# A two-layer decoder trunk on one core: which instructions keep their written order, and where lambda and 1/rms stand

## The chip, the cores and the metric

One NeuronCore of a Trainium2 chip runs the whole kernel. The metric is device microseconds (us) of one execution; before the change it is 1796.87 us, the median of 3 runs (1796.75 to 1797.68). The engines are called as the profile calls them: PE (TensorE, matmul), DVE (VectorE), ACT (ScalarE), POOL (GpSimd), and SP, whose queue issues nearly all DMA transfers.

## The reference, cut to what matters

```python
for l in range(DEPTH):                       # 2 layers, 512 tokens, width 1024
    h = rmsnorm(x, attn_norm[l])
    proj = h @ w_in[l]
    q_a, kv_a, g_a, q_b, k_b, v_b, uv_c = jnp.split(proj, IN_OFFSETS, axis=-1)
    o_a = nsa_attention(...)                 # compressed, selected and window branches
    o_b = diff_attention(...)                # two softmax maps per head, p0 - lam * p1
    o_c = chunked_sgu(uv_c, ...)             # u * (W_s @ rmsnorm(gelu(v)) + b)
    gates = sigmoid(h @ w_merge[l] + b_merge[l])
    x = x + (sum of gates * (o @ w_branch)) @ w_out[l]
    h = rmsnorm(x, ffn_norm[l])
    x = x + (silu(h @ w_ffn1[l]) * (h @ w_ffn3[l])) @ w_ffn2[l]
return rmsnorm(x, final_norm)
```

In `diff_attention`, `lam = exp(sum(lq1*lk1)) - exp(sum(lq2*lk2)) + lambda_init`, and q and k get rotary positions (tables of cosine and sine).

## The kernel before, in words

**Tiling.** Activations lie transposed: 8 tiles of 128 channels by 512 tokens. Weights stream from HBM as chunks of 128x1024 (`wr`, 4 buffers, L146). Each chunk is split in two fp32r halves: ACT makes the high part `wh` (L163), DVE or POOL the low part `wl` (L166), 3 buffers each. Every product takes three matmuls: `wh`·x high (L184), `wl`·x high (L185), `wh`·x low (L186); the lines L224 to L226 are the same where tokens are the output rows. Without the chunk's `wl` PE gets past one matmul of it only. An output bank in PSUM (`ps_g`, 3 buffers, or `ps_s`, 2) is free again when DVE or ACT has evacuated it.

**Start.** `setup` loads x and the first chunks and makes the split inputs `xg`. ACT squares the token-major copy of x (L311); `norm_r` turns the sums into 1/rms (`v` on DVE L482, `r` by a power on POOL L483); `norm_bcast` spreads it by four transposes on PE (L489) and a copy on ACT (L492) into `R`, by which every evacuation multiplies. The matmuls themselves don't need `R`.

**First tasks of a layer**, in the written order: `kvc` (chunks 0 and 1: compression inputs k and v), `u0`, `u1`, `u2` (chunks 2 to 4), `wk0` (chunk 5: 8 matmuls of the compression, lines L563 and L564), `u3` (chunk 6), `wk1` (chunk 7), `vv0` (chunk 8), and so on. In layer 0 the evacuations of `kvc` and `u0` are put off until `R` exists. The evacuation of k makes `xr` (L531), `xp` (L543) and the two halves `xh` (ACT L547, DVE L548), which `wk0` needs; that of v does the same again. `gelu_u` multiplies by `R` on DVE (L509) and applies gelu on ACT (L510). `loads` (called in `u1`) issues the SGU and compression constants (gn, sw, sgb, w2; L1297 to L1302) and in layer 0 also `loads2` (positions, the second parameter block `par`, and `lq`, L319 to L322). `setup2` computes lambda (`ex` L355 and L358, `nl`, `bh`, `sub`) and then the cosine and sine tables; it is written after `u3`.

**What sets the order.** The Python code writes the instructions; the framework's scheduler then orders each engine's queue, and may draw an instruction ahead of ones written earlier if nothing forbids it. Each engine works its queue off in that order. `pin` forbids: on DVE, ACT and POOL it chains every instruction from `first` on to the one before it. Before the change it is called once, after `u2` of layer 0, for all instructions since the first loads.

**The value task.** `V` (three chunks, four `ps` banks of 280 columns) ends in `v_evac`: per token tile ACT writes `v` high (L692) and the gates `ga` (L693), DVE `v` low (L694). The next task, a gate of branch c, needs the first of these banks. Nothing pins this place before the change. Near it stands the softmax of the compressed branch: its Exp on ACT (L795), then DVE's L799 to L806.

Of the kernel before, what the change touches and what calls it, by code (L numbers as in the profile page):

```python
# [80 lines left out]
class Kern:  # L81
    def __init__(self, tc, ctx, A):
        self.tc, self.nc, self.A = tc, tc.nc, A
        self.sb = ctx.enter_context(tc.tile_pool(name="sb", bufs=1))
        self.ps = ctx.enter_context(tc.tile_pool(name="ps", bufs=1, space=PSUM))
        self.dr = ctx.enter_context(tc.tile_pool(name="dr", bufs=1, space=DRAM))
        self.pending, self.timed = [], []
        self.now = self.clock = 0
        self.done = set()
        self.order = []  # L90
        self.raw, self.split = {}, {}
        self.n_dma = self.n_split = 0
# [141 lines left out]
    def setup(self):  # L234
# [32 lines left out]
        self.first = len(nc.cur_bb.bb.instructions)  # L267
# [45 lines left out]
        self.mark = len(nc.cur_bb.bb.instructions)  # L313

    def loads2(self):
# [3 lines left out]
        nc.sync.dma_start(self.pos_t, A["pos"])  # L319
        nc.sync.dma_start(self.par[1], A["par"][1])  # L320
# [24 lines left out]
    def setup2(self):  # L345

        nc = self.nc
        lq = self.lq.rearrange("p (l f d) -> p l f d", l=L, f=4)
        self.nlam, self.bh, self.sub = [], [], []
        for l in range(L):  # L350
            li = 0.8 - 0.6 * math.exp(-0.3 * l)
            ex = self.const(f"ex{l}", [P, 2])
            junk = self.t2("junk", (P, HD))
            for j in range(2):
                nc.vector.tensor_tensor_reduce(out=junk, in0=lq[:, l, 2 * j], in1=lq[:, l, 2 * j + 1],  # L355
                                               scale=1.0, scalar=0.0, op0=OP.mult, op1=OP.add,
                                               accum_out=ex[:, j:j + 1])
            nc.scalar.activation(ex, ex, AF.Exp)  # L358
            nl = self.const(f"nl{l}", [P, 1])
            nc.vector.scalar_tensor_tensor(nl, ex[:, 1:2], li, ex[:, 0:1], op0=OP.subtract, op1=OP.subtract)  # L360
            self.nlam.append(nl)
            bh = self.const(f"bh{l}", [P, 24])
            nc.vector.tensor_scalar(bh, self.par[l][:, P_BM:P_BM + 24], 0.5, None, op0=OP.mult)
            self.bh.append(bh)
            sub = self.const(f"sub{l}", [P, 1])
            nc.vector.tensor_scalar(sub, self.par[l][:, P_SUB:P_SUB + 1], 1.0 - li, None, op0=OP.mult)
            self.sub.append(sub)
        yield

# [71 lines left out]
        for j, tab in enumerate((self.cosT, self.sinT)):  # L441
            for h in range(4):
                nc.sync.dma_start(tab[32 * h:32 * h + 32, :], tab_d[j].rearrange("a b c -> a (b c)"))
        yield
# [242 lines left out]
    def v_evac(self, t, ps):  # L687
        nc = self.nc
        r = self.r4[:, t:t + 1]
# [6 lines left out]
        if t == TT - 1:  # L696
            nc.vector.tensor_scalar(self.ga, self.ga, 1.0, 0.5, op0=OP.add, op1=OP.mult)
# [569 lines left out]
    def layer_tasks(self, l):  # L1267
# [21 lines left out]
        def loads():  # L1289
            if l == 0:  # L1290
                self.loads2()
# [39 lines left out]
        def g_u(m):  # L1331
            hooks, ev = {}, self.gelu_u(m)
            if l == m == 0:
                ev = lambda ps, f=self.gelu_u(0): self.later(1002, lambda: f(ps), "ev")
            elif m == 1:
                hooks = {3: loads}
                if l == 0:
                    hooks.update({1: self.norm_bcast, 2: lambda: self.ensure("ev")})
            add("u%d" % m, [("u", m)], lambda i0: self.fm(i0, [ev], self.xg, hooks=hooks,
# [94 lines left out]
    def run(self):  # L1434
# [36 lines left out]
        for n, chunks, f, need in tasks:  # L1471
# [18 lines left out]
            if n == "u20":  # L1490
                self.pin(self.first, len(self.nc.cur_bb.bb.instructions))
        self.ensure()

# [104 lines left out]
```

## Time and profile before

| | before |
|---|---|
| median of 3 runs | 1796.87 us |
| profiled execution, its own time | 1797.58 us |
| its span in the profile | 1795.8 us (1.8 us lie around it) |
| PE busy | 1766.5 us, 98% of the span |
| DVE busy | 967.8 us, 54% |
| ACT busy | 748.5 us, 42% |
| POOL busy | 385.9 us, 21% |
| mean granted clock of PE | 0.995 of full speed |

PE's busy time and the span differ by some 29 us; that is all the time in which PE stood still. Matmuls of the trace overlap (the start of the next one lies before the modelled end of the last), so rates are read from start to start.

### The profile page before, as it was taken

To read this page: it belongs to the slowest core of one execution; us is meant where nothing else is said; L and a number is where in the kernel's file an instruction comes from. 1 tells how busy PE (TensorE), PEld (TensorE's weight loads), DVE (VectorE), ACT (ScalarE), POOL (GpSimd) and SP (SyncE) were. 2 spreads that over 40 slices of the span, in tenths; PEclk is the share of its full clock that TensorE was granted. 3 is DMA by queue.
4 is the path that set the end of the run, shared out by engine and by line. 5 is a ranking of instruction groups with operands and counts; after the bars stand their busy time and mean duration, and the time that the engine had idled before them with its cause. 6 is when DMAs were issued, how large, how long until landed. Compare 5 with 4: busy or idle time off the path is not lost.

```text
span 1795.8 us, 22823 instructions
## 1 busy us (share of the span) xinstructions
PE 1766.5 (98%) x8500; PEld 1473.7 (82%) x8500; DVE 967.8 (54%) x1755; ACT 748.5 (42%) x1313; POOL 385.9 (21%) x371
## 2 busy tenths in 40 slices
PE   7999999999999999999999999999999999999998
PEld 5888888888888888888888888888888888888887
DVE  5686675666554444433365776647655454444222
ACT  4546673444343223322234577634543332233221
POOL 0053342344330000000012343315433200000000
PEclk9999999999999999999999999999999999999999
DMA  6563125623232222223243711165323232222221
GB/s 245 173 189 109 53 71 154 185 84 129 94 106 94 97 103 94 94 98 125 106 147 129 227 51 61 59 193 159 141 71 106 94 105 95 101 99 94 95 104 48
DMA packets 68318, 205.78 MB, mean 115 GB/s; under 512 B 8944, under 2 KB 11376, under 8 KB 68208
## 3 DMA queue, kind: packets, MB, share of 16 engines
q1 hardware_dynamic: 68064, 204.29, 33.6%
q8 instruction: 67, 1.10, 0.2%
q14 instruction: 43, 0.35, 0.1%
q10 hardware_dynamic: 144, 0.04, 0.0%
HBM read 185.29 MB, written 19.01 MB: 114 GB/s over the span
## 4 chain that ended last, share of the span: by engine, by line
PE 90%; DVE 3%; ACT 2%; issue 2%; POOL 1%; DMA 1%; DVEq 0%; POOLq 0%; SPq 0%; ACTq 0%
PE ps_g L184 25%; PE ps_g L186 25%; PE ps_g L185 25%; PE ps_o L910 2%; PE ps_g L224 2%; PE ps_t L888 2%; PE ps_g L225 2%; PE ps_g L226 2%; PE ps_s L841 1%; PE ps_s L840 1%; PE ps_o L1010 1%; POOL mix L1094 1%; DVE wl L166 1%; DMA xtok<-in_xtok 1%; PE ps_o L226 1%
## 5 line engine op out<-in xcount | busy, mean ns | idle before, releaser
L163 ACT ACTIVATE wh<-wr 128x1024 fp32r<-128x1024 f32 (+2 forms) x320 | 315.0, 988 | 656.0 <-PE ps_g L186 373.4
L184 PE MATMUL ps_g<-xg,wh 128*128 128x512 f32 x1400 | 556.5, 398 | 4.6 <-DVE v L694 3.5
L185 PE MATMUL ps_g<-xg,wl 128*128 128x512 f32 x1400 | 547.7, 391 | 1.0 <-DVE wl L166 0.5
L186 PE MATMUL ps_g<-xg,wh 128*128 128x512 f32 x1400 | 547.9, 391 | 0.0
L166 DVE TENSOR_TENSOR wl<-wr,wh 128x1024 fp32r<-128x1024 f32 (+1 forms) x308 | 364.6, 1187 | 241.6 <-ACT wh L163 241.0
L186 PEld LDWEIGHTS ps_g<-xg,wh 128*128 128x128 f32 x1400 | 263.6, 188 | 55.7
L184 PEld LDWEIGHTS ps_g<-xg,wh 128*128 128x128 f32 x1400 | 264.1, 189 | 54.4 <-DVE v L694 4.0
L185 PEld LDWEIGHTS ps_g<-xg,wl 128*128 128x128 f32 x1400 | 264.2, 189 | 50.7 <-DVE wl L166 1.5
L831 ACT ACTIVATE e<-e,nm 128x128 f32<-128x128 f32 (+1 forms) x192 | 107.4, 560 | 99.1 <-DVE nm L829 95.5
L184 PE MATMUL ps_g<-act,wh 128*128 128x512 f32 (+1 forms) x374 | 141.1, 377 | 0.0
L185 PE MATMUL ps_g<-act,wl 128*128 128x512 f32 (+1 forms) x374 | 140.8, 376 | 0.0
L186 PE MATMUL ps_g<-act,wh 128*128 128x512 f32 (+1 forms) x374 | 140.8, 376 | 0.0
L466 POOL TENSOR_TENSOR acc<-acc,sq 128x512 f32<-128x512 f32 x18 | 29.4, 1631 | 381.1 <-ACT sq L465 381.1
L829 DVE CUSTOM_DVE_ANT_0 e<-ps_s,con 128x128 f32<-128x128 f32 (+1 forms) x192 | 91.8, 482 | 34.7 <-PE ps_s L841 26.1
L871 POOL TENSOR_SCALAR e<-e,sm,ga 128x256 f32<-128x256 f32 (+3 forms) x128 | 82.0, 651 | 127.3 <-DVE sm L867 108.6
L1151 DVE TENSOR_TENSOR fb<-ps_g,R 128x512 f32<-128x512 f32 x44 | 30.4, 691 | 128.8 <-PE ps_g L186 128.8
L166 POOL TENSOR_TENSOR wl<-wr,wh 128x512 fp32r<-128x512 f32 x48 | 73.2, 1525 | 98.4 <-ACT wh L163 87.0
L1142 DVE TENSOR_TENSOR fa<-ps_g,R 128x512 f32<-128x512 f32 x44 | 30.4, 691 | 95.3 <-PE ps_g L186 95.3
L184 PEld LDWEIGHTS ps_g<-act,wh 128*128 128x128 f32 x374 | 70.4, 188 | 13.0
L185 PEld LDWEIGHTS ps_g<-act,wl 128*128 128x128 f32 x374 | 70.4, 188 | 12.8
L186 PEld LDWEIGHTS ps_g<-act,wh 128*128 128x128 f32 x374 | 70.3, 188 | 12.8
L1194 POOL TENSOR_TENSOR acc<-acc,sq 128x512 f32<-128x512 f32 x5 | 6.9, 1382 | 316.6 <-ACT sq L1192 316.6
(244 smaller groups left out, 2580.2 us busy)
## 6 DMA issues: line engine op xcount, KB each, us to landing
wr<-in_wst SPq DMA_DIRECT2D x268, 512.0 KB, 3.3
rp_d<-pc SPq DMA_DIRECT2D x112, 128.0 KB, 3.0
wr<-in_wst SPq DMA_DIRECT2D x48, 256.0 KB, 2.6
q<-rp_d SPq DMA_DIRECT2D x16, 512.0 KB, 6.2
kh<-rp_d SPq DMA_DIRECT2D x24, 256.0 KB, 5.9
xT<-in_xT SPq DMA_DIRECT2D x8, 512.0 KB, 6.7
kl<-rp_d SPq DMA_DIRECT2D x12, 256.0 KB, 6.9
xtok<-in_xtok SPq DMA_DIRECT2D x4, 512.0 KB, 10.0
```

What stands on the lines that cost most here:

```text
L163: nc.scalar.activation(h[:, :w], t[:, :w], AF.Copy)
L166: eng.tensor_tensor(lo[:, a:b], t[:, a:b], h[:, a:b].bitcast(F32), op=OP.subtract)
L184: nc.tensor.matmul(out, wh[:, c], xh[:, ts], start=first, stop=False)
L185: nc.tensor.matmul(out, wl[:, c], xh[:, ts], start=False, stop=False)
L186: nc.tensor.matmul(out, wh[:, c], xl[:, ts], start=False, stop=last)
L224: nc.tensor.matmul(o, x[k][:, 0, ts], wh[:, sl], start=(k == 0), stop=False)
L225: nc.tensor.matmul(o, x[k][:, 0, ts], wl[:, sl], start=False, stop=False)
L226: nc.tensor.matmul(o, x[k][:, 1, ts], wh[:, sl], start=False, stop=(k == KT - 1))
L829: nc.vector.tensor_tensor_reduce(out=e[:, :n], in0=s[:, :n], in1=self.mask[:, S - n:], scale=-0.125, scalar=3e38, op0=OP.add, op1=OP.min, ...
L831: nc.scalar.activation(e[:, :n], e[:, :n], AF.Exp, bias=nm, scale=-1.0, accum_out=sm)
L871: nc.gpsimd.tensor_scalar(e[:, :n], e[:, :n], sm[:, h:h + 1], self.ga[:, i, b:b + 1], op0=OP.mult, op1=OP.mult)
L888: nc.tensor.transpose(pt[:, j - 2 * part, h, :], E[2 * v + h][:, j * P:(j + 1) * P], self.ident)
```

## The change

- `pin` no longer covers everything up to `u2`. The code now collects two kinds of ranges, the first loads (from the first `xg` to `norm_r`) and, in each layer, the value evacuations from the first to the last `v_evac`, and pins them at the end: inside a range the order holds, and all that is written later stays behind it.
- `norm_bcast` is called after the fourth of `u0`'s eight steps instead of in `u1`, and the put-off evacuations follow one step later; `u0`'s own evacuation is no longer put off.
- Lambda is written after the tables. `par` and `lq` are loaded in `loads3`, which is called with `loads`, and `loads` moves from `u1` to `u3`, in both layers; only the positions are loaded in `u1`.

```diff
@@ setup
-        self.first = len(nc.cur_bb.bb.instructions)
+        first = len(nc.cur_bb.bb.instructions)
...
         self.norm_r(ss)
-        self.mark = len(nc.cur_bb.bb.instructions)
+        self.pins.append((first, len(nc.cur_bb.bb.instructions)))
@@ loads2
         nc.sync.dma_start(self.pos_t, A["pos"])
+
+    def loads3(self):
+
+        nc, A = self.nc, self.A
         nc.sync.dma_start(self.par[1], A["par"][1])
         self.lq = self.t2("lq")
@@ setup2: the block from `lq = self.lq.rearrange(...)` to `self.sub.append(sub)` moves, unchanged, behind the tables
@@ v_evac
+        if t == 0:
+            self.v_first = len(nc.cur_bb.bb.instructions)
...
         if t == TT - 1:
+            self.pins.append((self.v_first, len(nc.cur_bb.bb.instructions)))
@@ g_u
-            hooks, ev = {}, self.gelu_u(m)
+            hooks = {}
             if l == m == 0:
-                ev = lambda ps, f=self.gelu_u(0): self.later(1002, lambda: f(ps), "ev")
-            elif m == 1:
-                hooks = {3: loads}
-                if l == 0:
-                    hooks.update({1: self.norm_bcast, 2: lambda: self.ensure("ev")})
+                hooks = {3: self.norm_bcast, 4: lambda: self.ensure("ev")}
+            elif m == 1 and l == 0:
+                hooks = {1: self.loads2}
+            elif m == 3:
+                hooks = {1: loads}
@@ run
-            if n == "u20":
-                self.pin(self.first, len(self.nc.cur_bb.bb.instructions))
         self.ensure()
+        for first, mark in self.pins:
+            self.pin(first, mark)
```

What the scheduler makes of it is seen in the queues. They differ from those of before at a few places only; three are shown. Line numbers in the changed kernel are a few higher (L485 there is L482 of before, L434 is L355, L437 is L358, L495 is L492, L550 is L547, L513 is L510, L697 is L692, L801 is L795, L837 is L831).

DVE at the end of the first loads (`v` is the first step to 1/rms, `ex`, `bh`, `sub` belong to lambda), before:

```order
L275 SCALAR_TENSOR_TENSOR xg<-xT,par_63,xg 128x512 x2
L166 TENSOR_TENSOR wl<-wr,wh 128x1024
L363 TENSOR_SCALAR bh_456<-par_64 128x24
L366 TENSOR_SCALAR sub_458<-par_64 128x1
L355 ISA junk,ex_438<-lq 128x64
L355 ISA ex_438 128x1
L355 ISA junk,ex_449<-lq 128x64
L355 ISA ex_449 128x1
L482 TENSOR_SCALAR v_158<-ss_153 128x4
L355 ISA junk,ex_438<-lq 128x64
```

and in the change:

```order
L166 TENSOR_TENSOR wl<-wr,wh 128x1024
L485 TENSOR_SCALAR v_158<-ss_153 128x4
L434 ISA junk,ex_595<-lq 128x64
L434 ISA ex_595 128x1
L442 TENSOR_SCALAR bh_602<-par_63 128x24
L445 TENSOR_SCALAR sub_604<-par_63 128x1
L434 ISA junk,ex_595<-lq 128x64
L434 ISA ex_595 128x1
L434 ISA junk,ex_606<-lq 128x64
L434 ISA ex_606 128x1
```

`v` has moved ahead of lambda; lambda itself has not moved behind the tables in the queue: it still stands ahead of the next weight split.

ACT from lambda's Exp to the first gelus, before:

```order
L358 ACTIVATE ex_449<-ex_449 128x2
L163 ACTIVATE wh<-wr 128x1024
L492 ACTIVATE R<-ps_t 128x512
L547 ACTIVATE xh<-xp 128x8x64 x4
L510 ACT_TABLE_LOAD
L510 ACTIVATE u<-u 128x512
L163 ACTIVATE wh<-wr 128x1024
L510 ACTIVATE u<-u 128x512
L163 ACTIVATE wh<-wr 128x1024 x3
```

and in the change:

```order
L437 ACTIVATE ex_606<-ex_606 128x2
L163 ACTIVATE wh<-wr 128x1024
L495 ACTIVATE R<-ps_t 128x512
L163 ACTIVATE wh<-wr 128x1024
L550 ACTIVATE xh<-xp 128x8x64 x2
L163 ACTIVATE wh<-wr 128x1024
L550 ACTIVATE xh<-xp 128x8x64 x2
L513 ACT_TABLE_LOAD
L513 ACTIVATE u<-u 128x512 x3
L163 ACTIVATE wh<-wr 128x1024 x3
```

The high parts of chunks 5 and 6 have moved ahead of the gelu of `u0`; DVE's low parts of both follow suit, each ahead of a pair of `xh`, and those of chunks 7 and 8 stand behind three `u` and the first six instructions of the tables.

ACT at the value evacuations of a layer (`ce` is the compressed branch's softmax; the 128x512 `wh` is a later chunk), before:

```order
L163 ACTIVATE wh<-wr 128x1024
L163 ACTIVATE wh<-wr 128x512
L692 ACTIVATE v_1126<-ps_g,r_159 128x4x64
L693 ACTIVATE ga<-ps_g,r4h 128x24
...
L693 ACTIVATE ga<-ps_o,r4h 128x24
L831 ACT_TABLE_LOAD
L831 ACTIVATE e,sm_1306<-e,nm 128x128 x2
```

and in the change:

```order
L163 ACTIVATE wh<-wr 128x1024
L697 ACTIVATE v_1126<-ps_g,r_159 128x4x64
L698 ACTIVATE ga<-ps_g,r4h 128x24
...
L698 ACTIVATE ga<-ps_o,r4h 128x24
L801 ACT_TABLE_LOAD
L801 ACTIVATE ce<-ce 128x512
L163 ACTIVATE wh<-wr 128x512
L837 ACTIVATE e,sm_1306<-e,nm 128x128 x2
```

The 128x512 split has moved from ahead of the evacuations to behind them, and the Exp of `ce`, which stood with a table load some fourteen instructions earlier, ahead of `hg` of the compression, now stands in between; `hg` needs no table load of its own any more. Layer 1 shows the same. On DVE the instructions from L799 on move behind the evacuations and the first logits (L829). On SP the loads of sw, sgb and w2 move behind two more weight chunks in layer 0 and one more in layer 1.

## Rows read from the trace of the kernel before

**Rows 1.** What PE waited for: total us, times, longest us.

```profile
PE ps_s L563 <- ACT wh L163: 6.5, 2, 6.3
PE ps_g L184 <- DVE v L694: 3.5, 2, 1.8
PE ps_t L581 <- ACT hg L577: 0.7, 1, 0.7
```

**Rows 2.** Timeline, PE, first 60 us: start, us, instruction, [idle before <- releaser].

```profile
25.84 0.50 PE L185 MATMUL ps_s<-xg,wl 128*128 128x512 f32 x1 [1.49 <-DVE wl L166]
...
36.89 0.39 PE L186 MATMUL ps_g<-xg,wh 128*128 128x512 f32 x1
43.62 0.58 PE L563 MATMUL ps_s<-wh,xh 128*128 128x256 f32 x1 [6.35 <-ACT wh L163]
...
56.47 0.40 PE L224 MATMUL ps_g<-wh,xg 128*128 128x512 f32 x1
```

**Rows 3.** Timeline, ACT, first 60 us.

```profile
20.34 1.06 ACT L163 ACTIVATE wh<-wr 128x1024 fp32r<-128x1024 f32 x1 [1.55 <-DMA wr<-in_wst]
24.53 0.35 ACT L358 ACTIVATE ex<-ex 128x2 f32<-128x2 f32 x2 [3.13 <-DVE ex L355]
...
27.74 0.60 ACT L492 ACTIVATE R<-ps_t 128x512 f32<-128x512 f32 x1 [1.92 <-PE ps_t L489]
...
42.53 1.04 ACT L163 ACTIVATE wh<-wr 128x1024 fp32r<-128x1024 f32 x1
```

**Rows 4.** Timeline, DVE, first 60 us.

```profile
23.90 0.23 DVE L355 CUSTOM_DVE_ANT_0 junk<-lq 128x64 f32<-128x64 f32 x1 [1.69 <-DMA lq<-in_lqk]
...
24.55 1.23 DVE L166 TENSOR_TENSOR wl<-wr,wh 128x1024 fp32r<-128x1024 f32 x1
...
28.37 1.75 DVE L531 TENSOR_TENSOR xr<-ps_g,R 64x256 f32<-64x256 f32 x4 [1.29 <-ACT R L492]
30.15 2.18 DVE L543 TENSOR_TENSOR xp<-xr,par 128x512 f32<-128x512 f32 x2
33.03 2.38 DVE L548 TENSOR_TENSOR xh<-xp,xh 128x512 fp32r<-128x512 f32 x2 [0.70 <-ACT xh L547]
...
39.95 1.29 DVE L548 TENSOR_TENSOR xh<-xp,xh 128x512 fp32r<-128x512 f32 x2 [0.69 <-ACT xh L547]
41.27 0.69 DVE L509 TENSOR_TENSOR u<-ps_g,R 128x512 f32<-128x512 f32 x1
...
51.34 0.29 DVE L379 TENSOR_SCALAR ang<-ang,con 128x128 f32<-128x128 f32 x1
...
89.58 0.68 DVE L636 TENSOR_TENSOR t<-ps_g,cosR 128x512 f32<-128x512 f32 x1
```

**Rows 5.** Timeline, POOL, first 80 us.

```profile
24.51 1.02 POOL L483 TENSOR_TENSOR r<-v,mhalf 128x4 f32<-128x4 f32 x1 [23.66 <-DVE ex L355]
...
32.96 1.30 POOL L708 TENSOR_TENSOR sw<-sw,con 128x512 f32<-128x512 f32 x1 [6.99 <-DMA sw<-in_swT]
75.79 1.30 POOL L499 TENSOR_TENSOR cosR<-cosT,R 128x512 f32<-128x512 f32 x1 [41.53 <-DMA cosT<-tab_d]
```

**Rows 6.** Busy us by stretch (PE, PEld, DVE, ACT, POOL), then granted clock, DMA share, GB/s.

```profile
45.00:60.00 15.00, 14.50 (x55) 11.62 (x56) 11.06 (x25) 6.63 (x8) 0.00 (x0) 0.75 0.46 156
141.00:145.00 4.00, 4.00 (x14) 3.34 (x13) 2.34 (x12) 2.51 (x7) 0.49 (x2) 0.57 0.87 263
```

**Rows 7.** Timeline, PE, behind the value task of layer 0, then of layer 1.

```profile
139.69 0.50 PE L184 MATMUL ps_g<-xg,wh 128*128 128x512 f32 x1 [1.77 <-DVE v L694]
...
145.51 0.28 PE L840 MATMUL ps_s<-kh,q 128*128 128x256 f32 x1
...
1022.78 0.50 PE L184 MATMUL ps_g<-xg,wh 128*128 128x512 f32 x1 [1.77 <-DVE v L694]
...
1027.60 0.28 PE L840 MATMUL ps_s<-kh,q 128*128 128x256 f32 x1
```

**Rows 8.** Timeline, ACT, at the value evacuations of layer 0.

```profile
137.96 0.63 ACT L163 ACTIVATE wh<-wr 128x512 fp32r<-128x512 f32 x1 [3.63 <-PE ps_o L226]
```

More of the change, by code (lines that the diff above doesn't have):

```diff
@@ L90, in __init__ @@
         self.order = []
-        self.raw, self.split = {}, {}
+        self.raw, self.split, self.pins = {}, {}, []
         self.n_dma = self.n_split = 0
@@ L347, in setup2 @@
         nc = self.nc
[L348 to L368, printed above, removed]
         slots = [self.t4("ang", [P, 8, P]) for _ in range(2)]
@@ L443, in setup2 @@
                 nc.sync.dma_start(tab[32 * h:32 * h + 32, :], tab_d[j].rearrange("a b c -> a (b c)"))
+        yield
+        lq = self.lq.rearrange("p (l f d) -> p l f d", l=L, f=4)
+        self.nlam, self.bh, self.sub = [], [], []
+        for l in range(L):
+            li = 0.8 - 0.6 * math.exp(-0.3 * l)
+            ex = self.const(f"ex{l}", [P, 2])
+            junk = self.t2("junk", (P, HD))
+            for j in range(2):
+                nc.vector.tensor_tensor_reduce(out=junk, in0=lq[:, l, 2 * j], in1=lq[:, l, 2 * j + 1],
+                                               scale=1.0, scalar=0.0, op0=OP.mult, op1=OP.add,
+                                               accum_out=ex[:, j:j + 1])
+            nc.scalar.activation(ex, ex, AF.Exp)
+            nl = self.const(f"nl{l}", [P, 1])
+            nc.vector.scalar_tensor_tensor(nl, ex[:, 1:2], li, ex[:, 0:1], op0=OP.subtract, op1=OP.subtract)
+            self.nlam.append(nl)
+            bh = self.const(f"bh{l}", [P, 24])
+            nc.vector.tensor_scalar(bh, self.par[l][:, P_BM:P_BM + 24], 0.5, None, op0=OP.mult)
+            self.bh.append(bh)
+            sub = self.const(f"sub{l}", [P, 1])
+            nc.vector.tensor_scalar(sub, self.par[l][:, P_SUB:P_SUB + 1], 1.0 - li, None, op0=OP.mult)
+            self.sub.append(sub)
         yield
@@ L1290, in loads @@
             if l == 0:
-                self.loads2()
+                self.loads3()
             sw = self.t4("sw", [P, 2, 4, P])
@@ L1331, in g_u @@
         def g_u(m):
-            hooks, ev = {}, self.gelu_u(m)
+            hooks = {}
             if l == m == 0:
-                ev = lambda ps, f=self.gelu_u(0): self.later(1002, lambda: f(ps), "ev")
-            elif m == 1:
-                hooks = {3: loads}
-                if l == 0:
-                    hooks.update({1: self.norm_bcast, 2: lambda: self.ensure("ev")})
-            add("u%d" % m, [("u", m)], lambda i0: self.fm(i0, [ev], self.xg, hooks=hooks,
+                hooks = {3: self.norm_bcast, 4: lambda: self.ensure("ev")}
[3 more added lines that the diff above has]
+                hooks = {1: loads}
+            add("u%d" % m, [("u", m)], lambda i0: self.fm(i0, [self.gelu_u(m)], self.xg, hooks=hooks,
                                                           tag="s" if l == 0 and m == 1 else "g"))
```

## The prediction

> **What bounds the kernel now.** PE is busy for 98% of the span, so a change of order can only win what PE stands still, some 29 us, and what it runs at the low clock. I read the list of PE's waits first: the longest is one wait of 6.3 us in the first compression task, put down to ACT's weight split; next come two equal waits behind the value evacuations and a small one on `hg` [rows 1]. The timeline then shows why. In the first 60 us PE ends `u2` at about 37.2, waits 6.35 us for the high part of chunk 5, and starts `vv0` only at 56.47 [rows 2]. From 45 to 60 us its mean granted clock is 0.75: with two levels, 2.4 and 1.2 GHz, half of that stretch ran at the lower one, after the long wait [rows 6]. The wait itself ends with ACT: the split at 42.53 [rows 3] stood in the pinned queue behind the gelu of `u0`, which waited for DVE's product at 41.27, which stood behind both rounds of `xr`, `xp` and `xh` [rows 4]. So DVE's work ahead of the split, not ACT's speed, ends last. Its late start has one cause: DVE waits until 23.90 for `lq` [rows 4], and the first step to 1/rms stands behind two of lambda's four products, so that the power on POOL begins at 24.51 [rows 5] and `R` at 27.74 [rows 3], which releases the evacuations at 28.37 [rows 4].
>
> **The change part by part.** The sum is made against the profiled execution, 1797.58 us, which is 0.7 above the median.
>
> *1/rms earlier, lambda not later.* `v` now runs when ACT's squares are done, and the transposes stand in `u0` ahead of PE's wait at 25.84. They cost PE what they cost before. But `R` gains little: in ACT's queue lambda's Exp and one weight split still stand ahead of its copy, and Exp still waits for `lq` at 23.90. The two `bh` and `sub` pairs now stand there too, about 0.2 us (estimate: four instructions of a few columns, each shorter than the 0.23 of a lambda product [rows 4]). The split of chunk 3, ready on ACT at 21.4 [rows 3], thus starts on DVE at about 24.8 instead of 24.55, and PE's wait of 1.49 us stays; it resumes some 1.3 us after that start, as before, at 26.1 instead of 25.84 [rows 2, 4]. `R` comes at about 26.6 instead of 28.3. That is no gain by itself, since DVE is busy with splits until after that.
>
> *The unpinned start.* This is the large term. I lay DVE's new queue end to end from 24.8, with durations from [rows 4]: two splits (1.23 each) and the two small `nl` to 27.4; `xr` 1.75, `xp` 2.18, to 31.3; split of chunk 5 to 32.6; `xh` 1.29 to 33.9; the second `xr` and `xp` to 37.8; split of chunk 6 to 39.0; `xh` to 40.3; three `u` of 0.69 to 42.4; six table instructions of up to 0.29 to 44.0; the splits of chunks 7 and 8 to 45.2 and 46.5. I take 46.2 for the last, because each duration overlaps the next start a little (two splits start 1.15 to 1.3 apart). ACT keeps up: its share in this stretch is shorter, and each split's high part now stands ahead of the `xh` or behind the last `u`.
>
> PE against it: `u2` ends at 37.2 plus the 0.25 lost above; chunk 5's low part has been there since 32.6 and `xh` since 33.9, so **the 6.35 us are gone**. `wk0` takes about 1 us at full clock. `u3` must wait for chunk 6 until 39.0, about 0.6 us; its 24 matmuls at 0.23 us start to start end at 44.3. `wk1` waits for chunk 7 to 45.2, and the second matmul of `vv0` for chunk 8 to 46.2. Before, that second matmul came 0.23 after 56.47. The gain at this point is 56.7 - 46.2 = 10.5 us. Of it 7.5 are waits and about 4 the low clock, less the new short waits. So DVE is what is late next.
>
> One thing speaks against this change. The loads of sw now follow chunk 10's, whose buffer comes free with the split of chunk 6, so sw lands around 44 to 45 and POOL's mask product of 1.30 us [rows 5] runs beside the splits of chunks 7 and 8. Before, it ran beside an `xh` pair, which took 2.38 instead of 1.29 us [rows 4, 5]. I take off 0.9 and keep **9.6 us**. The Trainium skill has this as a rule: in "SBUF — State Buffer", section "SBUF: two separate sides", a DVE instruction with two SBUF inputs and a GpSimd one that reads SBUF exclude each other for the whole instruction. By the rule the loss would be up to the full 1.30 us, and this term 9.2. The rows, at 1.09, stand nearer to the rule than to no loss, and the two answers differ by less than the rest of this term is uncertain.
>
> Further on PE is some 10 us ahead of before and the tables about 9 (their queue starts at 42.4 instead of 51, with two splits and the mask beside it). The margin was large: `cosR` began at 75.79 [rows 5], the first product with it at 89.58 [rows 4]. The moved loads of gn, sw and w2 have a similar margin; I cost both at nothing. If that cover were gone, `KR` would wait for the tables one for one.
>
> *Value evacuations, each layer.* PE waits 1.77 us for the first bank [rows 7], because ACT's evacuations stood behind a 128x512 split which waited until 137.96 for the last matmul of the value task, through its buffer [rows 8]. That split now stands behind them; the four banks finish one by one, so the first is evacuated while PE still computes the others: 1.77 us go, in both layers. In layer 0 the wait was followed by a lower granted clock, 0.57 over 4 us [rows 6]; from the gate's first matmul to the fourth logits took 5.82 us, against 4.82 in layer 1, where the clock held [rows 7]. I add that 1.0 in layer 0. New: DVE must wait there for the Exp of `ce` behind its table load, between the first and the second logits. By my laying out, PE reaches the fourth logits within 0.3 us of when DVE frees their bank. The 4.82 us already hold a wait of 0.3, so I take nothing off. **1.77 + 1.0 + 1.77 = 4.5 us**; bounds 2.5 (DVE's wait eats 1 us in each layer) and 5.1.
>
> *`hg` in layer 1.* ACT no longer loads a table ahead of it; the 0.7 us that PE waited [rows 1] go. The later loads of layer 1 cost nothing: POOL needs sw long after.
>
> Sum: 9.6 + 4.5 + 0.7 = 14.8 us; 1797.58 - 14.8 = 1782.8 for the profiled execution, and 1796.87 - 14.8 = **1782.0 us** for the median.
>
> **The rivals.**
> 1. *DVE becomes the bound for longer.* DVE's queue from 24 to 60 us has no idle time left, so each stretch of it falls on PE. For: `xh` has already been seen at 2.38 for 1.29, and the splits of chunks 11 and 12 stand three to five table instructions later. Against: later splits had some 3 us in hand. A tenth more over 22 us is 2.2 us, and late splits of two chunks another 2: 1786.2.
> 2. *The clock drops all the same.* Waits of 0.6, 0.9 and a few tenths remain close together. For: one wait of 1.77 us was enough in layer 0 [rows 6, 7]. Against: the same wait in layer 1, and the 1.49 us at 25.84, were not. The price is what the low clock cost before: about 4 us here, 1 in layer 0, so 1787. The Trainium skill, "TensorE: Matmul & The Clock Gate", section "A second HAM failure mode: psum-queue depth-cycling", says that many short idles between groups of matmuls can make the gate swing; by that rule this rival would be the likelier one, but the trace agrees with it in one place of three.
> 3. *Slower.* The heads of DVE's and ACT's queues now hang on `lq` with everything, 1/rms copy, splits and evacuations. Each us that `lq` lands later moves the whole chain by one. It decides from a landing at 23.9 + 14.8 = 38.7 us: beyond that the kernel is slower than before, at 45 us by 6 (1803). Against it: `lq` keeps its place in SP's queue, behind the same loads.
> 4. *The change does not do what it says.* Half of this is already in the sum: lambda is not behind the tables in the queue. Should its wait not hold the chain after all, splits and `R` would come 2 to 3 us earlier, PE's 1.49 us would go, and the short waits with them: 1778.5.
>
> **How the numbers follow.** Forecast 0.62, rival 1 0.17, rival 2 0.12, rival 3 0.02, rival 4 0.05, and 0.02 for gains that later waits eat whole. The forecast's own range is 1779.5 to 1785: 2.5 either way from the bounds of the start (8 to 10.5) and of the evacuations. To hold 8 in 10 it must take in rivals 1 and 2: 1777.8 to 1787.5. A measurement of this kernel tells about 0.2%, 3.6 us, from no change. Faster by more: all but rival 3 and the last case, 0.96; within: 0.02; slower: 0.02.
>
> **What would show it.** In the changed profile: PE's wait in L563 for ACT gone, and in its place waits under 1 us each for DVE's split at about 38, 44 and 46; PE's `vv0` at 46 to 47; granted clock 1.0 from 30 to 60 us; lambda's first product still at about 23.9 after an idle DVE since 19; POOL's power at about 19, but `R` only at about 26; no wait for L694 in either layer and none for `hg`. The prediction is wrong if `vv0` starts after 50 us, if the clock falls, or if gates and logits behind the value task take longer than the 4.8 us of layer 1.

## The result and the profile after

| | before | changed |
|---|---|---|
| median | 1797.04 us (4 runs, 1796.75 to 1797.68) | 1782.55 us (4 runs, 1782.41 to 1782.60) |
| ratio to before, 95% interval | | 0.9919 [0.9902, 0.9936] |
| profiled execution / its span | 1797.58 / 1795.8 us | 1782.41 / 1780.6 us |
| PE busy | 1766.5 us | 1761.3 us |
| DVE busy / ACT busy | 967.8 / 748.5 us | 966.1 / 743.8 us |
| mean granted clock of PE | 0.995 | 0.998 |

The change is worth 14.5 us by the medians and 15.2 by the two spans; the forecast was 14.8 and 1782.0 us. PE runs the same 8500 matmuls. Of the 15.2 us, 10.0 are time in which it stood still (29.3 before, 19.3 after, as span less busy time), and 5.2 are busy time, which I put down to the low clock of before. Again I begin with the list of PE's waits (total us, times, longest us), here of the changed kernel:

```profile
PE ps_s L846 <- DVE nm L835: 4.2, 4, 1.2
PE ps_s L185 <- DVE wl L166: 1.4, 1, 1.4
...
PE ps_s L567 <- DVE wl L166: 1.1, 1, 1.1
...
PE ps_g L185 <- DVE wl L166: 0.9, 3, 0.4
```

and one row of the same list of the kernel before, which answers to the first of these:

```profile
PE ps_s L840 <- DVE nm L829: 2.8, 3, 1.3
```

The three waits that the forecast named [rows 1] have no row any more: wk0 for ACT's split, the gate for `v`, `hg`. Two short ones for DVE's splits are new in the first 60 us, and the waits for `nm`, the softmax's evacuation, have grown from 2.8 to 4.2 us. The timeline of PE in the first 60 us (start, us, instruction, [idle before <- releaser]) shows where the short ones lie:

```profile
26.04 0.50 PE L185 MATMUL ps_s<-xg,wl 128*128 128x512 f32 x1 [1.35 <-DVE wl L166]
...
38.62 0.50 PE L185 MATMUL ps_g<-xg,wl 128*128 128x512 f32 x1 [0.40 <-DVE wl L166]
...
45.30 0.39 PE L567 MATMUL ps_s<-wl,xh 128*128 128x256 f32 x1 [1.06 <-DVE wl L166]
...
46.24 0.40 PE L224 MATMUL ps_g<-wh,xg 128*128 128x512 f32 x1
```

`vv0` starts at 46.24 in place of 56.47 [rows 2]. The granted clock (the last but two of the columns: PE, PEld, DVE, ACT, POOL busy, clock, DMA share, GB/s) is full from 45 to 60 us and behind the value task, where it was 0.75 and 0.57 [rows 6]:

```profile
45.00:60.00 15.00, 14.70 (x75) 12.57 (x76) 14.21 (x40) 5.24 (x7) 0.00 (x0) 1.00 0.54 181
...
127.00:133.00 6.00, 5.13 (x29) 4.14 (x28) 4.03 (x13) 3.98 (x10) 1.28 (x1) 1.00 0.76 229
```

DVE in the same stretch, timeline of the changed kernel:

```profile
18.80 0.17 DVE L485 TENSOR_SCALAR v<-ss 128x4 f32<-128x4 f32 x1 [3.56 <-ACT xtok L311]
23.89 0.22 DVE L434 CUSTOM_DVE_ANT_0 junk<-lq 128x64 f32<-128x64 f32 x1 [4.93 <-DMA lq<-in_lqk]
...
24.77 1.22 DVE L166 TENSOR_TENSOR wl<-wr,wh 128x1024 fp32r<-128x1024 f32 x1
...
27.20 1.74 DVE L534 TENSOR_TENSOR xr<-ps_g,R 64x256 f32<-64x256 f32 x4
...
32.19 1.29 DVE L551 TENSOR_TENSOR xh<-xp,xh 128x512 fp32r<-128x512 f32 x2
...
37.35 1.21 DVE L166 TENSOR_TENSOR wl<-wr,wh 128x1024 fp32r<-128x1024 f32 x1
...
42.16 0.23 DVE L366 TENSOR_SCALAR ang<-ang 128x128 int32<-128x128 int32 x1
...
42.76 1.35 DVE L366 TENSOR_SCALAR ang<-ang 128x128 int32<-128x128 int32 x1
44.03 2.35 DVE L166 TENSOR_TENSOR wl<-wr,wh 128x1024 fp32r<-128x1024 f32 x2
```

From 23.89 to 45 it is busy for all but 0.3 us; the last row is the splits of chunks 7 and 8, for which PE waits at 45.30. The first `L366` takes 0.23 us, the second 1.35. Beside the second runs POOL's mask product, as its timeline shows:

```profile
19.12 1.02 POOL L486 TENSOR_TENSOR r<-v,mhalf 128x4 f32<-128x4 f32 x1 [18.27 <-DVE v L485]
...
42.73 1.29 POOL L714 TENSOR_TENSOR sw<-sw,con 128x512 f32<-128x512 f32 x1 [22.22 <-DMA sw<-in_swT]
```

The new wait behind the value task of layer 0, in the timelines of PE (the gate's first matmul, the fourth logits), DVE, ACT and POOL:

```profile
127.50 0.39 PE L184 MATMUL ps_g<-xg,wh 128*128 128x512 f32 x1
...
132.67 0.39 PE L846 MATMUL ps_s<-kh,q 128*128 128x256 f32 x1 [0.87 <-DVE nm L835]
...
130.32 0.69 DVE L805 TENSOR_REDUCE csm<-ce 128x16 f32<-128x512 f32 x1 [1.14 <-ACT ce L801]
...
131.33 0.87 DVE L809 TENSOR_TENSOR csm<-csm,ga 128x16 f32<-128x16 f32 x1
...
132.33 0.28 DVE L835 CUSTOM_DVE_ANT_0 e<-ps_s,con 128x128 f32<-128x128 f32 x1
...
129.65 0.63 ACT L801 ACTIVATE ce<-ce 128x512 f32<-128x512 f32 x1
...
130.88 1.28 POOL L166 TENSOR_TENSOR wl<-wr,wh 128x512 fp32r<-128x512 f32 x1 [12.21 <-ACT wh L163]
```

The gate no longer waits (1.77 before [rows 7]). But DVE waits 1.14 us for the Exp of `ce`, which ends late because a table load stands ahead of it, and the product in L809 ends only when POOL's split has ended, at 132.16. All that time the second logits hold their bank, and PE wants it for the fourth.

The clearest account compares places that both kernels pass. Layer 1's rows of after are those of the gate and the fourth logits again:

```profile
1007.16 0.39 PE L184 MATMUL ps_g<-xg,wh 128*128 128x512 f32 x1
...
1012.33 0.39 PE L846 MATMUL ps_s<-kh,q 128*128 128x256 f32 x1 [0.87 <-DVE nm L835]
```

| PE at | before [rows 2, 7] | after | ahead by | won in the stretch | forecast |
|---|---|---|---|---|---|
| `vv0` | 56.47 | 46.24 | 10.23 | 10.2 | 9.6 |
| gate, layer 0, its wait taken off | 137.92 | 127.50 | 10.42 | 0.2 | 0 |
| fourth logits, layer 0 | 145.51 | 132.67 | 12.84 | 2.4 | 2.8 |
| gate, layer 1, its wait taken off | 1021.01 | 1007.16 | 13.85 | 1.0 | 0.7 (`hg`) |
| fourth logits, layer 1 | 1027.60 | 1012.33 | 15.27 | 1.4 | 1.8 |
| end (the spans) | 1795.8 | 1780.6 | 15.2 | -0.1 | 0 |

### The profile page after: what moved, and what is told of

Its sections match the earlier page's. It is cut to its first block, busy times and chain, and to the rows that moved or that the text cites. A ratio compares the mean times of both kernels' runs of the same rounds, so it can differ in the third digit from the quotient of the medians.

```text
span 1780.6 us, 22816 instructions
## 1 busy us (share of the span) xinstructions
PE 1761.3 (99%) x8500; PEld 1470.1 (83%) x8500; DVE 966.1 (54%) x1755; ACT 743.8 (42%) x1309; POOL 386.0 (22%) x371
## 4 chain that ended last, share of the span: by engine, by line
PE 91%; DVE 3%; ACT 2%; issue 2%; DMA 1%; POOL 1%; DVEq 0%; POOLq 0%; SPq 0%; ACTq 0%
PE ps_g L184 25%; PE ps_g L185 25%; PE ps_g L186 25%; PE ps_o L916 2%; PE ps_g L224 2%; PE ps_t L894 2%; PE ps_g L225 2%; PE ps_g L226 2%; PE ps_s L847 1%; PE ps_s L846 1%; PE ps_o L1016 1%; POOL mix L1100 1%; DVE wl L166 1%; DMA xtok<-in_xtok 1%; PE ps_o L226 1%
## 5 line engine op out<-in xcount | busy, mean ns | idle before, releaser
L837 ACT ACTIVATE e<-e,nm 128x128 f32<-128x128 f32 (+1 forms) x192 | 107.4, 560 | 99.5 <-DVE nm L835 95.8
```

Of the source, the lines that this page charges most:

```text
L837: nc.scalar.activation(e[:, :n], e[:, :n], AF.Exp, bias=nm, scale=-1.0, accum_out=sm)
```

## The experiments

Twelve kernels ran. "Won" is the median of the kernel before, taken on the same chip in the same set of runs, less the kernel's own. The intervals are wide, about 0.15% either way (2.7 us). Runs of one kernel lie within 0.5 us of each other in six of the twelve; in e1, e3, e4, e10, e11 and c4 they spread over 1.2 to 2.0 us. So two of my kernels that differ by 1 to 3 us are compared by their traces first, each of which is one execution, and by the medians beside them.

| kernel | median us | won | ratio to before, 95% interval |
|---|---|---|---|
| e1 value evacuations kept in order, nothing else | 1792.84 | 4.7 | 0.9973 [0.9962, 0.9984] |
| e2 the change without them | 1787.42 | 10.1 | 0.9944 [0.9929, 0.9959] |
| e3 the change with the long kept order | 1789.44 | 8.1 | 0.9956 [0.9941, 0.9971] |
| e4 the change with 1/rms in `u1` again | 1782.28 | 15.3 | 0.9915 [0.9899, 0.9932] |
| e5 the change, lambda held behind the tables | 1780.65 | 16.7 | 0.9907 [0.9892, 0.9922] |
| e7 the change, loads in `vv1` | 1782.32 | 15.0 | 0.9917 [0.9900, 0.9933] |
| e9 the change, sum of `ce` later | 1780.22 | 17.1 | 0.9905 [0.9890, 0.9920] |
| c3 e5, e7 and e9 together | 1777.89 | 19.4 | 0.9892 [0.9877, 0.9907] |
| e10 before, order kept to `norm_r` only | 1787.26 | 10.5 | 0.9944 [0.9927, 0.9960] |
| e11 before, loads moved only | 1796.29 | 1.4 | 0.9993 [0.9984, 1.0003] |
| c4 c3, tables later | 1777.54 | 20.2 | 0.9891 [0.9877, 0.9906] |
| e13 before with the two kept ranges only | 1781.92 | 15.3 | 0.9914 [0.9897, 0.9930] |

My theory was that two independent things make the gain: the order freed behind the first loads (about 10 us), and the order kept at the value evacuations (4 to 5). The rivals were that 1/rms earlier or the moved loads do it, and that the two parts depend on each other.

**e1, the value evacuations alone.** To the kernel before:

```diff
+        if t == 0:
+            self.v_first = len(nc.cur_bb.bb.instructions)
...
         if t == TT - 1:
+            self.pins.append((self.v_first, len(nc.cur_bb.bb.instructions)))
...
         self.ensure()
+        for first, mark in self.pins:
+            self.pin(first, mark)
```

> The kernel before with only the pins of the value evacuations added. Theory (start and value terms are independent): 1.77 us of PE's wait for v go in each layer, about 1 us at the low clock in layer 0, 0.7 for hg, less a new wait of about 0.9 in each layer for the Exp of ce: 3.4 to 5, so 1792 to 1793.6. In the trace the wait for L563 of 6.3 us stands as before. Rival A (the gain behind the values depends on the earlier start, for instance on later chunks that then arrive in time): under 2 us of gain, above 1795. Rival B (the value pins are worth the whole of my term and more, so that the start is worth less than 10): under 1791.

1792.84 us, 4.7 won: the theory. The wait of 6.4 us in `wk0` stands, those for `v` and `hg` are gone, and the wait of 0.88 for the fourth logits is there in both layers. It came with this part of the change, not with the earlier start.

**e2, the start alone.** From the changed kernel, one line out:

```diff
-            self.pins.append((self.v_first, len(nc.cur_bb.bb.instructions)))
```

> The changed kernel without the pins of the value evacuations. Theory: vv0 starts at 46.2 us as in the changed kernel, the 10.2 us of the start are kept to the end, and the waits for v (1.77 in each layer) and hg (0.7) are back: 1797.0 - 10.2 = 1786.8, plus or minus 0.8. Together with the run that has the value pins alone the two gains should add up to 14.5. Rival (part of the start's gain is given back later, because an engine that is earlier only waits longer for a transfer or for another engine): above 1789.

1787.42 us, 10.1 won; with e1 that makes 14.8, against 14.5 for the whole change. The two parts add up within what the runs can tell. One thing I had not expected stands behind the value task of layer 0, on PE's timeline and in the window:

```profile
129.63 0.50 PE L184 MATMUL ps_g<-xg,wh 128*128 128x512 f32 x1 [1.77 <-DVE v L699]
...
134.44 0.28 PE L845 MATMUL ps_s<-kh,q 128*128 128x256 f32 x1
...
128.00:136.00 8.00, 6.06 (x30) 4.91 (x31) 4.50 (x18) 6.04 (x18) 2.15 (x3) 1.00 0.76 257
```

PE waits the same 1.77 us as before, yet the clock holds at 1.00, and gate to fourth logits takes 4.81 us in place of 5.82. But the 1.0 us is not won: the same rows of layer 1, where the clock held before, show that it is lost there instead.

```profile
1011.71 0.50 PE L184 MATMUL ps_g<-xg,wh 128*128 128x512 f32 x1 [1.77 <-DVE v L699]
...
1017.53 0.28 PE L845 MATMUL ps_s<-kh,q 128*128 128x256 f32 x1
...
1010.00:1018.00 8.00, 6.29 (x24) 5.28 (x25) 4.05 (x16) 5.51 (x16) 2.16 (x3) 0.79 0.78 260
```

Here gate to fourth logits takes 5.82 us, against 4.82 before [rows 7], and from 1012 to 1017 us the granted clock is 0.66. Each of the four traces that keep both waits of 1.77 us shows one such stretch: layer 0 before the change and in e10 (5.84), layer 1 in e2 and in e11 (5.84). None of the ten with the value evacuations in order shows it; their clock is 1.00 in both places. So the 1.0 us goes with the two waits, and with the value term, and the earlier start only moved it from one layer to the other.

**e3, the long order again.** From the changed kernel, the range of the first loads runs to `u2` as before:

```diff
-        first = len(nc.cur_bb.bb.instructions)
+        self.first = len(nc.cur_bb.bb.instructions)
...
-        self.pins.append((first, len(nc.cur_bb.bb.instructions)))
...
+            if n == "u20":
+                self.pin(self.first, len(self.nc.cur_bb.bb.instructions))
```

> The changed kernel, but with the order kept from the first loads through u2 of layer 0, as before; the earlier 1/rms, the later loads and the value pins stay. Theory (the start's gain is the freed order): the high part of chunk 5 stands behind u's gelu again, PE waits 5 to 6.5 us in wk0, and the time is 1791 to 1793.5, as with the value pins alone. Rival (1/rms made earlier is what brings the gain, since everything up to u2 hangs on R): vv0 starts 5 us or more earlier than in the kernel before and the time is below 1788.

1789.44 us: neither. Against e1 it wins 3.4 us where I had expected none, and the wait ahead of `wk0` was not there at all. Only short ones for splits followed, of 0.43, 1.11 and 0.45 us. PE had spent the long wait earlier, as its timeline and a window show:

```profile
25.59 1.12 PE L491 MATMUL ps_t<-con,r 128*128 128x128 f32 x4 [4.13 <-POOL r L485]
...
24.00:32.00 8.00, 6.41 (x20) 5.25 (x21) 6.92 (x20) 2.60 (x6) 1.38 (x4) 0.58 0.52 173
```

The transposes of 1/rms now stand early in PE's queue, and the kept order holds the first step to it behind lambda's wait for `lq`, so PE waits 4.13 us there and runs behind it at the low clock, from 26 to about 30 us, in place of the low stretch after 45. `vv0` starts at 52.49, 4.0 earlier than before. On DVE, the first product of `u0` starts at 39.23 instead of 41.27 [rows 4]: 1.0 because `R` comes at 26.75 instead of 27.74 [rows 3], 1.1 because `xh` takes 1.29 instead of 2.38. The other 2 us I put down to the shorter low stretch, which is argued from the trace and was not tried by itself. What e3 does show is that 6.4 to 6.9 us (e3 against the changed kernel, by the column "won" and by the medians) hang on the long order being gone.

**e4, 1/rms in the second group again.** From the changed kernel:

```diff
-            hooks = {}
+            hooks, ev = {}, self.gelu_u(m)
             if l == m == 0:
-                hooks = {3: self.norm_bcast, 4: lambda: self.ensure("ev")}
+                ev = lambda ps, f=self.gelu_u(0): self.later(1002, lambda: f(ps), "ev")
             elif m == 1 and l == 0:
-                hooks = {1: self.loads2}
+                hooks = {1: lambda: (self.norm_bcast(), self.loads2()), 2: lambda: self.ensure("ev")}
...
```

> The changed kernel with 1/rms spread in the second u group again and u0's evacuation put off again, as before; order kept as in the changed kernel. Theory (R is not what ends last: DVE is busy with splits until about 27): vv0 within 1 us of 46.2 and the time within 1.5 us of the changed kernel's, 1781 to 1784. Rival (1/rms early is needed for the gain): R comes at 28 or later, the chain of xr, xp, xh and the splits of chunks 6 to 8 moves by 1.5 us or more, and the time is 1784.5 or more.

1782.28 us: no difference. `R` is copied at 28.86, 2.9 us later than in the changed kernel, and `vv0` starts at 46.46, 0.2 later. The earlier call of `norm_bcast` is worth nothing that can be measured; while it was late, DVE did splits.

**e10, the kept range shortened and nothing else.** To the kernel before:

```diff
-            if n == "u20":
-                self.pin(self.first, len(self.nc.cur_bb.bb.instructions))
         self.ensure()
+        self.pin(self.first, self.mark)
```

> The kernel before with one edit: the kept order ends at norm_r, at the end of the first loads, instead of after u2. 1/rms is spread in u1, lambda and its loads and the SGU's loads are written where they were, no value pins. Freed, the queue draws the first step to 1/rms ahead of lambda and the splits of chunks 5 to 8 ahead of the gelus by itself. Theory (the freed order is the whole start term, the moved calls are worth nothing by themselves): as the run without value pins, 1787 plus or minus 0.8, wait of 6.3 us in wk0 gone. Rival (the calls moved in the code bring part of it, as the 3.4 us suggest that the long order with those calls kept over the value pins alone): 1789.5 or more.

1787.26 us (1786.23 to 1788.26), 10.5 won, as e2 within the spread of its runs: one edit is the whole start term. Its DVE and PE rows:

```profile
18.77 0.17 DVE L482 TENSOR_SCALAR v<-ss 128x4 f32<-128x4 f32 x1 [3.57 <-ACT xtok L311]
...
45.49 0.40 PE L224 MATMUL ps_g<-wh,xg 128*128 128x512 f32 x1
```

Freed, the scheduler itself draws `v` ahead of lambda, and puts the loads of sw, sgb and w2 behind two more chunks, although the code writes both where it did before.

**e11, the loads alone.** To the kernel before:

```diff
-                hooks = {3: loads}
...
+            elif m == 3:
+                hooks = {1: loads}
```

with par and `lq` in `loads3`, as in the change.

> The kernel before with only the loads moved (SGU loads, par and lq from u1 to u3); the long kept order, 1/rms in u1 and lambda ahead of the tables as before. In the chip's order only SP's queue and a few table instructions differ. Theory (POOL's mask product beside xh costs DVE 1.1 us on the path to the split that PE waits for): xh of k takes 1.29 instead of 2.38, PE's wait of 6.3 us in wk0 becomes 5.2, the time is 1.0 to 1.3 us less, 1796. Rival A (this is what made the 3.4 us of the run with the long order): 1793.5 to 1794.5. Rival B (the mask product then falls on the splits of chunks 7 and 8 and takes it back): within 0.5 us of before.

1796.29 us; the interval of the ratio holds 1, so the sign is not settled by the times. The trace shows the price I had guessed, and that it is paid again later:

```profile
42.56 0.58 PE L567 MATMUL ps_s<-wh,xh 128*128 128x256 f32 x1 [5.33 <-ACT wh L163]
...
47.75 3.44 DVE L166 TENSOR_TENSOR wl<-wr,wh 128x1024 fp32r<-128x1024 f32 x2
```

The wait in `wk0` is 5.33 in place of 6.35 us: without the mask product beside it `xh` takes 1.29. Now the product runs beside two splits, which take 3.44 in place of the 2.35 they take above, and `vv0` starts only 0.46 earlier than before.

**e13, the two kinds of ranges, nothing moved.** To the kernel before: the edits of e1 and e10 together.

> The kernel before with the two kinds of ranges alone: order kept from the first loads to norm_r, and over the value evacuations in each layer. 1/rms is spread in u1, lambda and all loads are written as before. Theory (the two ranges are the whole change in time): 1782.4 plus or minus 1, as the changed kernel, the sum of what each kind won alone (10.4 and 4.7) off 1797.5. Rival (1/rms in u0 or the later loads matter once the order is free): 1784 or more.

1781.92 us: as fast as the changed kernel. The moved lambda, the moved loads and the earlier 1/rms are worth nothing that can be measured.

Next, the three places at which the forecast had said that something still ends last. **e5, lambda really late.** From the changed kernel:

```diff
+    def hold(self, first, mark):
+        last, ins = {}, self.nc.cur_bb.bb.instructions
+        for i in ins[:first]:
+            last[i.engine] = i
+        for i in ins[first:mark]:
+            if i.engine in (mybir.EngineType.DVE, mybir.EngineType.Activation):
+                self.tc.add_manual_dep(i, last[i.engine].name, mybir.DependencyInfo(
+                    mybir.DependencyClass.NoSync, mybir.DependencyReason.DATA), reason="order")
...
+        self.hold(*self.lam)
```

(`lam` is the range of lambda's instructions.)

> The changed kernel with lambda's instructions on DVE and ACT really held behind the tables (in the changed kernel they are only written there). Theory (lambda's wait for lq is what still ends last on DVE at the start): DVE no longer waits to 23.9 us, the split of chunk 3 starts at about 21.5, PE's wait of 1.35 us at 26.0 goes, R comes some 2 us earlier, and PE's short waits of 0.4 and 1.06 us for the splits of chunks 6 and 7 shrink or go. PE can win 1.35 to 2.8 us: 1779.6 to 1781.1. Price against it: one more pair of table loads of 1.28 us on ACT ahead of hg, up to 1 us. Rival (PE is fed late by the transfers of the chunks, or by DVE's sum of work, so lambda's place does not matter): within 0.7 us of the changed kernel.

1780.65 us, 1.9 below the changed kernel. DVE and then PE, timelines:

```profile
21.54 1.23 DVE L166 TENSOR_TENSOR wl<-wr,wh 128x1024 fp32r<-128x1024 f32 x1 [2.41 <-ACT wh L163]
...
40.87 1.32 DVE L369 CAST ang<-pos 128x128 f32<-128x128 int32 x1
...
43.70 0.50 PE L225 MATMUL ps_g<-wl,xg 128*128 128x512 f32 x1 [0.64 <-DVE wl L166]
...
47.28 0.50 PE L224 MATMUL ps_g<-wh,xg 128*128 128x512 f32 x1 [0.79 <-DVE u L524]
```

The split starts 3.2 us earlier (24.77 above), the waits of 1.35, 0.40 and 1.06 us are gone, and `vv0` starts at 42.67, 3.6 earlier. By `hg` 2.0 of that is given back: PE now waits for the split of chunk 8, behind a cast that took 1.32 us beside POOL's mask product, and for an evacuation that stands behind table instructions. So lambda's wait was what ended last, and where it is gone PE's next waits stand behind DVE's table instructions.

**e7, the loads one task later.** From the changed kernel, `loads` of layer 0 is called in `vv1`:

```diff
-            elif m == 3:
+            elif m == 3 and l == 1:
                 hooks = {1: loads}
...
-                lambda i0: self.tm(
+                lambda i0: (loads() if l == 0 and c == 1 else None) or self.tm(
```

> The changed kernel with the loads of gn, sw, sgb, w2, par and lq of layer 0 issued one task further on, in vv1. Theory (POOL's mask product, beside DVE's small table instruction that took 1.35 us in place of 0.22, holds up the splits of chunks 7 and 8): the mask product moves behind those splits, PE's wait of 1.06 us in wk1 goes, vv0 starts at about 45.2, and the time is 1.0 us less, 1781.0 to 1781.8. Rival (that instruction was long for another reason): the 1.35 us stays where it was and the time is the changed kernel's.

1782.32 us: no gain. The long instruction is short again, but the splits start no earlier:

```profile
42.69 0.22 DVE L366 TENSOR_SCALAR ang<-ang 128x128 int32<-128x128 int32 x1
...
43.89 2.35 DVE L166 TENSOR_TENSOR wl<-wr,wh 128x1024 fp32r<-128x1024 f32 x2
...
51.60 1.27 DVE L390 SCALAR_TENSOR_TENSOR ang<-ang 128x128 f32<-128x128 f32 x1
```

The scheduler put eleven table instructions ahead of the splits of chunks 7 and 8 instead of six, and filled the time that the mask product had left. The rival said that the 1.35 us would stay; it did not. But what the mask product costs PE in the changed kernel was not shown by this run, because the order changed with it.

**e9, the sum of `ce` behind the next logits.** From the changed kernel, `hold` (of e5) over DVE's instructions of that sum:

```diff
+            first = len(nc.cur_bb.bb.instructions)
             sm = self.small("csm", 16, 1)
...
+            if g == 0:
+                self.holds.append((first, len(nc.cur_bb.bb.instructions)))
...
+        for first, mark in self.holds:
+            self.hold(first, mark)
```

> The changed kernel with one rule more: on DVE, the sum over the compressed branch's Exp and what follows it stand behind the second and third logits instead of ahead of the second, in both layers; no other queue differs. Theory (PE's new wait of 0.87 us for the bank of the fourth logits is DVE waiting for the Exp of ce, then held up beside POOL's split): the wait goes in both layers, 1.5 to 1.75 us, so 1780.6 to 1781.0, and the gain of the value term is then the forecast 4.5 or more. Rival (PE would have waited there anyway, for ACT's or DVE's work on the logits): the wait moves to a later place and the time is within 0.5 us of the changed kernel's.

1780.22 us, 2.3 below the changed kernel by medians and by spans. PE, then DVE, in layer 0:

```profile
131.67 0.28 PE L859 MATMUL ps_s<-kh,q 128*128 128x256 f32 x1
...
132.05 0.68 DVE L816 TENSOR_REDUCE csm<-ce 128x16 f32<-128x512 f32 x1
...
133.06 0.18 DVE L820 TENSOR_TENSOR csm<-csm,ga 128x16 f32<-128x16 f32 x1
```

The fourth logits start 1.0 us earlier, without a wait, and the product that took 0.87 beside POOL's split takes 0.18 behind it. The gain is larger than the two waits, 1.74 together: a matmul that restarts after a wait takes 0.39 us where one that follows takes 0.28, and PE's next logits came 1.2 us earlier, not 0.87.

**c3, all three.**

> The three edits before in one kernel. If they add up: 1777 (2.3 by lambda, 1.0 by the later loads, 1.7 by the later sum, off 1782.4). The first two win partly the same waits, those of wk1 and u3, so I expect 1777.5 to 1779.5. Rival (DVE's queue of the tables becomes late, the splits of chunks 11 and 12 behind it first): above 1780.

1777.89 us, as expected: `vv0` starts at 42.53 and its wait for chunk 8 is gone, which was behind the cast beside the mask product in e5. So here the later product does take a wait away. What that is worth in time is not shown: against the changed kernel c3 wins 4.7 us by the medians and 4.2 by the spans, e5 and e9 together 4.2 and 3.9, and the difference is no more than what runs of one kernel differ by.

**c4, the tables later still.** To c3, `hold` over the first six table instructions (`tab`):

```diff
-        for first, mark in self.holds + [self.lam]:
+        for first, mark in self.holds + [self.lam, self.tab]:
```

> The kernel with the three edits (lambda late, loads in vv1, sum later) and one more: the first six instructions of the tables on DVE stand behind u3's own evacuation, so that the splits of chunks 7 to 9 and that evacuation do not wait for tables. Theory: PE's wait of 0.6 us for u's evacuation at 46 us and the restarts behind it go, 0.5 to 1.0 us: 1776.9 to 1777.4. Rival (the tables now come late for the next splits or for the Exp of lambda ahead of hg): 1778 or more.

1777.54 us, not told apart from c3 (its span is 0.6 shorter). The wait for `u` is gone and `vv0` runs without any, but `hg` now comes late: on ACT the Sin of the tables, lambda's Exp with a table load of 1.28 us and a weight split stand ahead of it and of its own table load. The row of PE's waits:

```profile
PE ps_t L598 <- ACT hg L594: 1.5, 1, 1.5
```

c3 and c4 beat both kernels: 0.9891 of the time before for c4, where the change has 0.9919. The two intervals still touch, but every run of c4 (up to 1779.47) lies below every run of the change (from 1782.41). To put lambda's Exp behind `hg` would be the next step; it was not tried.

## Why the prediction was right, step by step

**The start** was the large term, and its mechanism is shown: e10 wins 10.5 us with the shorter range alone, and e3 loses 6.4 to 6.9 us with the long one. The forecast for `vv0` was 46 to 47; it is 46.24. Lambda's first product stands at 23.89, 1/rms on POOL at 19.12, `R` at 25.94, all as forecast, and the waits of 0.40 and 1.06 us stand where I expected 0.6 and 0.9, the second just over the "under 1 us" that I had named. The third, for chunk 8 in `vv0`, did not come: its split ends at 46.38, in time for the second matmul. The term was 0.6 too small. I had laid DVE's queue out end to end, though each instruction overlaps the next a little: `xr` starts at 27.20, not 27.4, the split of chunk 6 ends at 38.56, not 39.0, and the tables start at 41.58, not 42.4.

**The mask product** cost DVE 1.1 us, near the 0.9 that I took off, but not where I thought: it started at 42.73, since sw landed earlier than my 44 to 45, and held up one table instruction (1.35 for 0.23) ahead of the splits, not the splits. The Trainium skill, "SBUF — State Buffer", section "SBUF: two separate sides", lets a GpSimd instruction and a DVE one that needs the shared port exclude each other for the whole instruction; the trace agrees, since both DVE instructions that were held, at 42.76 and at 131.33, end within 0.1 us of POOL's end. That such a loss reaches PE is shown by PE's waits in e11 and in c3 beside e5, not by e7; what it costs PE in the changed kernel stays open.

**1/rms earlier is no gain by itself**: e4 and e13 confirm it. **Lambda not later**: its price is what e5 wins, 1.9 us. Rival 4 had set it at 3.5; 3.6 is what PE wins at `vv0`, but I had priced it at that place and not followed it to the next split and evacuation; by `hg` 2.0 of it are gone.

**The value evacuations** are the mis-sized term: 2.4 and 1.4 us measured, 3.8 together, where I had 4.5. The prediction had named as a sign of being wrong that gates and logits behind the value task take longer than the 4.8 us of layer 1, and they do: 5.17 us in both layers, 0.35 too long in each. The step that failed is "I take nothing off" for DVE's wait behind the Exp of `ce`. I had found the wait and laid it out, but not that POOL's split of 128x512, which now starts right behind ACT's, would hold up a tiny product on DVE: without those 0.69 us, by my estimate, DVE would have freed the bank within the margin that I had named (0.87 - 0.69 = 0.18, against 0.3). e9 takes the wait away and wins 2.3 us; with it the term exceeds my upper bound of 5.1. The 1.0 in this term, the low clock in layer 0, did come back, and e2 bears me out that it belongs here: the earlier start alone only moves the low stretch to layer 1. I had read layer 1 as a place where the clock holds; e2 and e11 show that it can fall there as well.

**`hg`** no longer waits, and the stretch that holds it won 1.0 where I had 0.7. The rest lies close by: PE's lead over the kernel before grows by 0.8 at `hg` itself and by 0.2 at a matmul of the value task 1.8 us later, which shows as a restart before (0.39 us for 0.29) and not after; why it restarts there I did not find out. That the start and `hg` came out too small (0.6 and 0.3) and the evacuations too large (0.7) is why the sum lies so near; that these errors cancel is luck.

**The rivals.** DVE did become the bound for longer, with 14.21 of 15 us busy, but its queue had just enough room, and no split behind chunk 8 was late. The low clock did not come back: 1.00 up to 1700 us, with waits of 1.35, 0.40 and 1.06 us within 20 us. The Trainium skill, "TensorE: Matmul & The Clock Gate", section "A second HAM failure mode: psum-queue depth-cycling", has one kernel in which frequent short idles between groups of matmuls made the gate swing. These three idles did not; whether more of them would, no run here shows. `lq` landed at 23.89, as before, so the slower case had no start.

## What to carry to other kernels

An order that is kept over a long chain makes every feed written behind it, here the weight splits, wait for the whole chain: keep it only where the scheduler's own order loses, and test each range alone, since here two ranges were the whole gain and the moved code nothing that could be measured. Before you credit an edit with a stretch that got faster, look whether the loss has moved: in e2 the low clock left layer 0 and came back in layer 1. Code that is written later has not moved until the queue shows it, and an instruction that is moved takes its neighbours with it: when you move one that DVE or POOL works on, lay out the other of the two as well, since here each was held up beside the other (0.87 us for 0.18, 1.35 for 0.23 on DVE). Price a short wait by the next place that PE passes, not by its listed length: 0.87 us listed cost 1.2.

## What the runs showed of the hardware that I had not expected

The same wait of PE was followed by different clocks. After 1.77 us behind the value task of layer 0 the granted clock was 0.57 before the change and 1.00 in e2; in layer 1 it was the other way round, 1.00 before and 0.66 in e2. At the start it held after 1.79 us in e13 and fell after 1.81 in e4, as these two windows show, e13 first:

```profile
24.00:32.00 8.00, 6.21 (x30) 5.00 (x29) 7.77 (x23) 2.90 (x5) 0.00 (x0) 1.00 0.65 228
```

```profile
24.00:32.00 8.00, 6.19 (x23) 4.78 (x22) 6.94 (x22) 2.90 (x5) 0.00 (x0) 0.79 0.63 204
```

The length of a wait near 1.8 us alone thus does not tell whether the clock falls; what decides was not found out. It need not be the kernel: the profiled execution of e4 took 1783.11 us at a mean clock of 0.997, the other three 1781.92 to 1782.37 at 0.998 to 0.999, and there is no trace of those. And the mask product was itself held up by DVE: 2.08 us in e5 against 1.29 in the changed kernel. It starts while a split runs on DVE until 40.96, and then it is DVE's cast that ends with it. POOL's timeline:

```profile
40.03 2.08 POOL L726 TENSOR_TENSOR sw<-sw,con 128x512 f32<-128x512 f32 x1 [19.35 <-DMA sw<-in_swT]
```
